# New engine and rank tables for the list scheduler of a two-layer hybrid backbone, and a price for PE's changes of tile shape

## The chip, the cores and the metric

The kernel runs on one core of one Trainium2 chip. The metric is the device time of one launch in microseconds. The core's engines each work through an instruction stream of their own in program order: TensorE (PE, with its weight loads listed as PEld), VectorE (DVE), ScalarE (ACT), GpSimd (POOL) and SyncE (SP), which issues the DMAs. They meet at semaphores.

## The reference, cut to what matters

Two layers work on 1024 latent tokens and 256 context tokens of width 1024, all in float32.

```python
for i in range(DEPTH):                                # 2 layers
    sh1, sc1, ga1, sh2, sc2, ga2 = split(silu(c) @ w_ada[i] + b_ada[i], 6)     # the context has its own
    hx = rms_norm(x, g_mix[i]) * (1 + sc1) + sh1      # hc the same from ctx
    zx = hx @ w_in[i]                                 # columns: q 512, k 128, v 128, pooling 256, Fourier 256
    q = apply_rope(head_rms(q, q_gain)); k = apply_rope(head_rms(k, k_gain))
    mx = concat([softmax(q k^T / 8) v over context + latent keys,    # 8 query heads of 64, 2 key heads
                 pool_mix(...), fourier_mix(...)])
    x = x + ga1 * (mx @ w_out[i])
    fx = rms_norm(x, g_ffn[i]) * (1 + sc2) + sh2
    gate, up = split(fx @ w_gate_up[i])               # 2816 columns each
    x = x + ga2 * ((silu(gate) * up) @ w_down[i])
    # layer 0 does the same for ctx, whose queries see context keys alone
return x
```

## The kernel before

Each large float32 product is made of three products of rounded halves, low by high, high by low, high by high (`mm3`, L485 to L487), summed in PSUM. So an operand is needed twice: as its rounded copy (the high half: a cast, `copy` at L472 on ACT and DVE, L470 on POOL) and as the remainder (the low half: a subtraction, `combine` at L475, on DVE or POOL). Weights come by DMA in tiles `hs` (output projection), `wst` (input projection, gate/up, down; `w` holds halves of them), `ast` (modulation). Some products are done in seven instead of eight partial products, for which sums of weight tiles and of inputs are made first (`ws`). The halves lie in `half`, `parts` and `w`.

A layer runs through input projection (`ps_in`), with the Fourier and pooling mixers; attention; output projection (`ps_o`) with the residual at L1883; gate and up (`ps_s`, `ps_m`, `ps_c` for the context); and down projection (`ps_d`, residual L2351). Between these, products for the modulation of the next steps (`ps_ada`, L591, 128 by 32 tiles) are put in.

Attention goes over blocks of 128 queries, and in each over four heads at a time, twice. Four heads are two pairs, and each head has 256 context keys and 1024 latent keys. The steps and their names are:

- SC, SA, SB: score products on PE (L1537), `ps_sc` for context keys, `ps_s` for latent keys
- MC, ML: row maxima on DVE (L1548, L1450); N: the exponential's bias on DVE (L1454)
- EC, EL: exponentials on ACT (L1460 into `pc` or `pd`, L1466 into `p`), with the row sums; EL gives back the score area in PSUM
- R: sum and reciprocal on DVE (L1554, L1555)
- Y and Z: scaling of `pc`/`pd` (128x256) and of `p` (128x1024) by the reciprocal (L1473 on ACT, L1475 on DVE or POOL)
- T: transposes on PE (L1488) into `ps_t`; C: copies `pt<-ps_t` (L472)
- V: products with the values on PE (L1512, 128 by 64 tiles) into `ps_pv`, in two runs per four heads; O: copy `mix<-ps_pv`

The order is found by a list scheduler in the kernel's own Python, the class `Plan`. Every step is recorded as an operation with a duration from a formula, what it comes after, and the buffers it takes and gives back. Its rank is a due time plus an entry of `SHIFTS` for its layer and name. Some kinds of step (copies, subtractions, scalings) may run on several engines: `ENGINES` lists these by the step's name (A for ACT, D for DVE, G for POOL). `run()` then keeps a clock for each engine, picks the step that can start first, of those that start nearly together the one with the lowest rank, gives it the engine on which it would start, and emits it. Steps on DVE and POOL exclude each other in that plan (`held`) unless named in `ALONE`. The hardware knows nothing of the plan's times: the instructions run in the order emitted on each engine, and wait for semaphores.

A run of value products is charged `4 * len(bs) * ns_fp32(256) + NS_MODE`, where `NS_MODE` stands for what PE loses when it changes from 128 by 128 tiles to other ones and back.

Of the kernel before, what the change touches and what calls it, by code (L numbers as in the profile page):

```python
# [39 lines left out]
H = {256: [f"h{k}" for k in range(8)], 768: [f"h{k}" for k in range(8, 16)], 0: [f"h{k}" for k in range(16, 20)]}  # L40
# [3 lines left out]
C = ("c0", "c1", "c2", "c3")  # L44
# [8 lines left out]
class Plan:  # L53
# [12 lines left out]
    SLACK = 60  # L66
    WINDOW = 40
# [38 lines left out]
    def run(self):  # L106
# [58 lines left out]
        pick = strict = True  # L165
        place = {e: k for k, e in enumerate(("PE", "A", "D", "G", "S", "N"))}
        while left:
# [26 lines left out]
            at, _, o, got, e = pick  # L194
            for b in o.can:
                ready[b].remove(o)
            o.engine, o.ns = e, o.can[e]
            by = o.engine
# [56 lines left out]
NS_MODE = 350  # L255
# [21 lines left out]
def setting(table, name, default):  # L277
# [6 lines left out]
             T=5.9, C=-12.1, H=-63.6, G=-21.5, V=6.3, F=6.6, O=-117.4, A=-149.8, X=-3.3)  # L284
# [6 lines left out]
ENGINES = {"C": "AD", "G": "G", "H": "ADG", "O": "A", "Y": "AD", "Z": "ADG", "act hi": "A", "act lo": "DG", "act sum": "D",  # L291
# [6 lines left out]
           "mix sum": "DG", "norm hi": "ADG", "norm lo": "G", "norm shift": "ADG", "out hi": "A", "out lo": "DG",  # L298
# [4 lines left out]

SHIFTS = ({"C": 919100, "EC": -545700, "EL": -1073100, "MC": -4100900, "ML": 314500, "N": -759500, "O": -2444400,
           "R": -2036600, "SA": 235500, "SB": -740400, "SC": -579700, "T": -221600, "V": -416700, "Y": 278400,
           "Z": 895000, "aa": -841600, "act hi": -1263600, "act lo": -1492900, "act sum": 1970600, "ada": -662600,
           "ada add": -132000, "ada row": -2031800, "ada sum": 1686900, "ada total": -365600, "ada turn": -1712000,
           "as": 1429200, "channels": -726100, "dft": -3497700, "dft alt": 1352500, "dft alt out": -676500,
           "dft copy": 1691400, "dft ctx": -1491300, "dft ctx out": -1510600, "dft out": 768100, "down": 1481200,
# [2187 lines left out]
```

## Time and profile before

| | |
|---|---|
| median of 3 runs | 2603.08 us (2601.51 to 2606.92) |
| profiled execution | 2608.01 us, span 2605.9 us |
| granted TensorE clock, mean | 0.991 |
| busy: PE, PEld | 2531.5 us (97%), 2092.5 us (80%) |
| busy: DVE, ACT, POOL | 2091.2 us (80%), 1253.5 us (48%), 540.2 us (21%) |
| chain that ended last | PE 78%, DVE 14%, ACT 3%, DMA 2%, issue 2% |

The span is what the profiler's records cover; the profiled execution's time is 2.1 us more, and the timed runs are executions without the profiler. A busy share is an average over stages with different limits, so that a stage's own limit is read from a window. In the 40 slices of the page PE stands at 9 tenths or more nearly throughout; the layer-0 stages end, read from the tiles written, near 238 us (input projection), 515 (attention), 615 (output projection), 1205 (gate and up), and layer 1's attention runs from about 1630 to 1870.

### The profile page before, as it was taken

The numbers are of one execution on the slowest core, as the hardware profiler recorded it, in microseconds if no ns is written. First come the engines' busy times: TensorE is split into PE (matmuls) and PEld (weight loads), VectorE is DVE, ScalarE is ACT, GpSimd is POOL, SyncE is SP. The second block draws the span as 40 slices with busy tenths as digits, with TensorE's granted clock in tenths as the row PEclk, the third lists the DMA queues.
The fourth block names the chain that finished last, engine by engine and source line by source line (L and its number), as shares of the span: only waits on it lengthen the run. The fifth ranks groups of instructions, "written<-read, shape, count | busy, mean of one in ns | idle before, by whom it ended". The sixth has DMA issues, their size and how long they took to land.

```text
span 2605.9 us, 38612 instructions
## 1 busy us (share of the span) xinstructions
PE 2531.5 (97%) x14382; PEld 2092.5 (80%) x14382; DVE 2091.2 (80%) x3466; ACT 1253.5 (48%) x2319; POOL 540.2 (21%) x450
## 2 busy tenths in 40 slices
PE   6999999998999999999999999999998999999999
PEld 5887777787788888888888988777776888888887
DVE  6766877799866998876788987877799977777886
ACT  4324888746322222224444533899746333334442
POOL 2022222122200000000223313322132311111241
PEclk9999999999999999999999999999998999999999
DMA  8243200354224455448434333100352423225733
GB/s 296 84 130 109 75 1 1 114 182 131 96 91 146 154 164 169 145 156 291 148 97 125 105 93 101 39 1 1 99 183 87 158 107 115 81 98 213 231 95 124
DMA packets 126203, 314.83 MB, mean 121 GB/s; under 512 B 14784, under 2 KB 23360, under 8 KB 126016
## 3 DMA queue, kind: packets, MB, share of 16 engines
q1 hardware_dynamic: 126016, 312.36, 36.4%
q8 instruction: 114, 1.87, 0.3%
q14 instruction: 73, 0.60, 0.1%
HBM read 244.94 MB, written 62.13 MB: 118 GB/s over the span
## 4 chain that ended last, share of the span: by engine, by line
PE 78%; DVE 14%; ACT 3%; DMA 2%; issue 2%; POOL 0%; SPq 0%; DVEq 0%; ACTq 0%; POOLq 0%
PE ps_s L485 8%; PE ps_s L486 8%; PE ps_s L487 8%; PE ps_d L485 6%; PE ps_d L486 6%; PE ps_d L487 6%; PE ps_pv L1512 5%; PE ps_t L1488 4%; PE ps_s L1537 4%; DVE half L475 3%; PE ps_in L485 3%; PE ps_in L486 3%; PE ps_in L487 3%; DVE x L1883 2%; DVE ws L475 1%
## 5 line engine op out<-in xcount | busy, mean ns | idle before, releaser
L472 ACT CAST half<-ws 128x512 fp32r<-128x512 f32 x404 | 243.9, 620 | 524.0 <-PE ps_s L487 236.6
L486 PE MATMUL ps_s<-half 128*128 128x512 f32 x1056 | 413.8, 392 | 6.4 <-DVE half L475 6.4
L485 PE MATMUL ps_s<-half 128*128 128x512 f32 x1056 | 414.8, 393 | 3.2 <-ACT half L472 2.6
L487 PE MATMUL ps_s<-half 128*128 128x512 f32 x1056 | 412.5, 391 | 0.0
L485 PE MATMUL ps_d<-half 128*128 128x512 f32 (+1 forms) x792 | 290.7, 367 | 2.0 <-ACT half L472 2.0
L486 PE MATMUL ps_d<-half 128*128 128x512 f32 (+1 forms) x792 | 290.2, 366 | 0.5 <-DVE half L475 0.5
L487 PE MATMUL ps_d<-half 128*128 128x512 f32 (+1 forms) x792 | 290.1, 366 | 0.0
L475 DVE TENSOR_TENSOR half<-ws,half 128x512 fp32r<-128x512 f32 x354 | 243.2, 706 | 56.6 <-ACT half L472 55.2
L486 PEld LDWEIGHTS ps_s<-half 128*128 128x128 f32 x1056 | 199.4, 189 | 50.7 <-DVE half L475 9.0
L485 PEld LDWEIGHTS ps_s<-half 128*128 128x128 f32 x1056 | 199.2, 189 | 46.6 <-ACT half L472 3.4
L487 PEld LDWEIGHTS ps_s<-half 128*128 128x128 f32 x1056 | 199.4, 189 | 41.6
L472 ACT CAST half<-wst 128x512 fp32r<-128x512 f32 x224 | 132.6, 618 | 163.9 <-PE ps_s L487 82.8
L475 POOL TENSOR_TENSOR ws<-wst 128x512 f32<-128x512 f32 x72 | 107.2, 1489 | 500.2 <-DVE half L475 413.8
L475 DVE TENSOR_TENSOR ws<-wst 128x512 f32<-128x512 f32 x258 | 173.4, 689 | 9.6 <-DMA wst<-in_w_gate_up 4.9
L475 DVE TENSOR_TENSOR half<-wst,half 128x512 fp32r<-128x512 f32 x204 | 152.3, 770 | 35.8 <-ACT half L472 35.6
L485 PEld LDWEIGHTS ps_d<-half 128*128 128x128 f32 x792 | 150.1, 190 | 26.7 <-ACT half L472 2.4
L486 PEld LDWEIGHTS ps_d<-half 128*128 128x128 f32 x792 | 150.1, 190 | 24.8 <-DVE half L475 0.7
L475 POOL TENSOR_TENSOR half<-ws,half 128x512 fp32r<-128x512 f32 x56 | 76.5, 1365 | 449.8 <-ACT half L472 396.2
L487 PEld LDWEIGHTS ps_d<-half 128*128 128x128 f32 x792 | 150.0, 189 | 24.0
L1450 DVE TENSOR_REDUCE smalls<-ps_s 128x1 f32<-128x1024 f32 x128 | 153.9, 1213 | 10.1 <-PE ps_s L1537 10.0
L485 PE MATMUL ps_in<-parts,w 128*128 128x512 f32 (+1 forms) x416 | 158.8, 382 | 1.6 <-ACT parts L472 1.6
L1512 PE MATMUL ps_pv<-pt,v 128*64 128x256 f32 x1312 | 156.4, 384 | 0.0
(284 smaller groups left out, 5874.0 us busy)
## 6 DMA issues: line engine op xcount, KB each, us to landing
wst<-in_w_gate_up SPq DMA_DIRECT2D x99, 512.0 KB, 4.3
ast<-in_w_ada SPq DMA_DIRECT2D x96, 512.0 KB, 3.7
as<-act_spill SPq DMA_DIRECT2D x165, 256.0 KB, 2.7
hs<-in_w_out SPq DMA_DIRECT2D x96, 256.0 KB, 3.0
act_spill<-c SPq DMA_DIRECT2D x44, 512.0 KB, 4.1
wst<-in_w_down SPq DMA_DIRECT2D x44, 512.0 KB, 6.4
x_spill<-x SPq DMA_DIRECT2D x28, 512.0 KB, 3.1
x<-x_spill SPq DMA_DIRECT2D x26, 512.0 KB, 6.5
```

What stands on the lines that cost most here:

```text
L472: (nc.scalar.copy if e == "A" else nc.vector.tensor_copy)(out, x)
L475: (nc.vector if e == "D" else nc.gpsimd).tensor_tensor(out, x, y, op)
L485: nc.tensor.matmul(o, wl, xh, start=start, stop=False)
L486: nc.tensor.matmul(o, wh, xl, start=False, stop=False)
L487: nc.tensor.matmul(o, wh, xh, start=False, stop=stop)
L1450: nc.vector.tensor_reduce(self.pair.col(1, self.h), self.s, AX.X, ALU.max)
L1488: nc.tensor.transpose(self.t[:, 2 * q + h, :], src, ident)
L1512: nc.tensor.matmul(self.bank[own], v[:, own], self.pt[k0][:, g, 2 * P * q:2 * P * q + 2 * P], start=(k0 + q == 0), stop=(k0 + q == self.nk ...
L1537: nc.tensor.matmul(o, self.q[0][:, self.h0 + h, :], kv["k", k0](self.g, j), start=(j == 1), stop=(j == 0))
L1883: nc.vector.scalar_tensor_tensor(v, o(), s, v, ALU.mult, ALU.add)
```

## The change

The change has three parts. The scheduler charges 300 ns (`SWITCH`) whenever PE goes from ordinary steps to one named in `PARTED`, and again when it goes back; `NS_MODE` falls from 350 to 50. The table `ENGINES` is new: the scaling of p (Z) may run on POOL alone, where it could run on ACT, DVE or POOL; the copy of attention results (O) may run on DVE too; `act sum` may go to POOL, `norm lo` goes from POOL to DVE, the high halves of the seventh and eighth columns of the input projection go to DVE, and others gain or lose an engine. Both tables of `SHIFTS`, one for a layer, are new in nearly every entry. What is computed stays the same.

```diff
+    SWITCH = 300
+    PARTED = ("ada", "V")
...
         pick = strict = True
+        parted = False
...
             o.engine, o.ns = e, o.can[e]
+            if e == "PE" and (o.name in Plan.PARTED) != parted:
+                parted, o.ns = not parted, o.ns + Plan.SWITCH
...
-NS_MODE = 350
+NS_MODE = 50
...
-ENGINES = {"C": "AD", "G": "G", "H": "ADG", "O": "A", "Y": "AD", "Z": "ADG", "act hi": "A", "act lo": "DG", "act sum": "D",
+ENGINES = {"C": "AD", "G": "G", "H": "ADG", "O": "AD", "Y": "AD", "Z": "G", "act hi": "A", "act lo": "DG", "act sum": "DG",
...
-           "R": -2036600, "SA": 235500, "SB": -740400, "SC": -579700, "T": -221600, "V": -416700, "Y": 278400,
-           "Z": 895000, "aa": -841600, "act hi": -1263600, "act lo": -1492900, "act sum": 1970600, "ada": -662600,
+SHIFTS = ({"C": 240000, "EC": -323700, "EL": -2200800, "MC": -481500, "ML": -539000, "N": -522600, "O": -598400, "R": -494400,
+           "SA": -45800, "SB": -1660200, "SC": -2264600, "T": -45500, "V": -777500, "Y": 141800, "Z": 256000,
```

In the changed kernel lines stand 3 to 6 later than before (L1466 is L1472, L1473 is L1479, L1475 is L1481, L475 is L481).

The first place is the steady part of layer 0's attention. On ACT, before, between two exponentials of latent scores:

```order
L1466 ACTIVATE p,smalls<-ps_s,smalls,rq 128x1024
L1473 ACTIVATE pd<-pd,smalls 128x256 x2
L1473 ACTIVATE p<-p,smalls 128x1024
L472 COPY mix<-ps_pv 128x2x128
L1460 ACTIVATE pc,smalls<-ps_sc,smalls,rq 128x256
L472 COPY pt<-ps_t 128x512
L1466 ACTIVATE p,smalls<-ps_s,smalls,rq 128x1024
```

And on ACT in the changed kernel:

```order
L1472 ACTIVATE p,smalls<-ps_s,smalls,rq 128x1024
L1479 ACTIVATE pd<-pd,smalls 128x256
L478 COPY mix<-ps_pv 128x2x128
L1466 ACTIVATE pc,smalls<-ps_sc,smalls,rq 128x256
L478 COPY pt<-ps_t 128x512
L1472 ACTIVATE p,smalls<-ps_s,smalls,rq 128x1024
L478 COPY pt<-ps_t 128x512 x2
```

The scaling of p is gone from ACT, and one of the two scalings of `pd`; POOL's stream has two scalings of p for each pair instead. On DVE at the same place, before:

```order
L1454 SCALAR_TENSOR_TENSOR smalls<-smalls,nrq 128x1
L1450 TENSOR_REDUCE smalls<-ps_s 128x1
L1475 TENSOR_SCALAR p<-p,smalls 128x1024
L1454 SCALAR_TENSOR_TENSOR smalls<-smalls,nrq 128x1
L472 CAST qt<-mix 64x256 x2
L472 COPY pt<-ps_t 128x512 x2
L1548 TENSOR_REDUCE smalls<-ps_sc 128x2
L1554 TENSOR_TENSOR smalls<-smalls 128x2
L1555 RECIPROCAL smalls<-smalls 128x2
L1450 TENSOR_REDUCE smalls<-ps_s 128x1
L1454 SCALAR_TENSOR_TENSOR smalls<-smalls,nrq 128x1
```

And on DVE in the changed kernel:

```order
L1561 RECIPROCAL smalls<-smalls 128x2
L1460 SCALAR_TENSOR_TENSOR smalls<-smalls,nrq 128x1
L1456 TENSOR_REDUCE smalls<-ps_s 128x1
L478 CAST qt<-mix 64x256 x2
L1460 SCALAR_TENSOR_TENSOR smalls<-smalls,nrq 128x1
L478 COPY pt<-ps_t 128x512 x2
L1554 TENSOR_REDUCE smalls<-ps_sc 128x2
L1456 TENSOR_REDUCE smalls<-ps_s 128x1
L1560 TENSOR_TENSOR smalls<-smalls 128x2
L1561 RECIPROCAL smalls<-smalls 128x2
L1460 SCALAR_TENSOR_TENSOR smalls<-smalls,nrq 128x1
```

The row maximum, which stood between the reciprocal and the bias, now stands ahead of the reciprocal, and the scaling of p is gone from DVE.

The second place is POOL from layer 0's output projection to its first gate products (`hs` and `wst` are weights as loaded, `ws` sums of them or of inputs). Before:

```order
L470 TENSOR_SCALAR w<-wst 128x512 x2
L470 TENSOR_SCALAR half<-x 128x512
L470 TENSOR_SCALAR w<-wst 128x512
L475 TENSOR_TENSOR ws<-x 128x512 x2
L470 TENSOR_SCALAR half<-ws 128x512
L470 TENSOR_SCALAR w<-wst 128x512 x2
L470 TENSOR_SCALAR half<-x 128x512
L475 TENSOR_TENSOR ws<-x 128x512
L470 TENSOR_SCALAR half<-x 128x512
L470 TENSOR_SCALAR half<-ws 128x512
```

And in the changed kernel:

```order
L481 TENSOR_TENSOR half<-hs,half 128x512
L481 TENSOR_TENSOR parts<-mix,parts 128x256
L481 TENSOR_TENSOR half<-hs,half 128x512 x4
L481 TENSOR_TENSOR half<-ws,half 128x512
L481 TENSOR_TENSOR half<-wst,half 128x512
L481 TENSOR_TENSOR half<-ws,half 128x512
L481 TENSOR_TENSOR half<-wst,half 128x512 x7
L481 TENSOR_TENSOR half<-ws,half 128x512
```

Casts (one input) and sums of x have left POOL for ACT and DVE, and subtractions (two inputs) have come from DVE.

The third place is PE at the entry of layer 0's attention, from the last score products among the input projection's. Before:

```order
L1537 MATMUL ps_s<-kd,qs 128x512 x8
L591 MATMUL ps_ada<-ast,cond 32x128 x8
L1031 MATMUL ps_v<-ident,vf 128x128 x6
L1537 MATMUL ps_sc<-kd,qs 128x256 x4
L604 MATMUL ps_at<-ident,rows 128x8
L1031 MATMUL ps_v<-ident,vf 128x128 x4
L1537 MATMUL ps_s<-kd,qs 128x512 x4
L1488 MATMUL ps_t<-ident,pc 128x128 x4
L591 MATMUL ps_ada<-ast,cond 32x128 x8
L1488 MATMUL ps_t<-ident,p 128x128 x12
```

And in the changed kernel:

```order
L1543 MATMUL ps_sc<-kd,qs 128x256 x4
L597 MATMUL ps_ada<-ast,cond 32x128 x8
L1494 MATMUL ps_t<-ident,pc 128x128 x4
L1543 MATMUL ps_s<-kd,qs 128x512 x4
L491 MATMUL ps_in<-parts,w 128x512
L492 MATMUL ps_in<-parts,w 128x512
L493 MATMUL ps_in<-parts,w 128x512
L491 MATMUL ps_in<-parts,w 128x512
L492 MATMUL ps_in<-parts,w 128x512
L493 MATMUL ps_in<-parts,w 128x512
L1494 MATMUL ps_t<-ident,p 128x128 x8
```

Six products of the input projection, which stood ahead of the last of these scores, now stand between scores and the first transposes of p.

## Rows read from the trace of the kernel before

**Rows 1.** The page: busy time of each engine, and the chain that ended last by engine.

```profile
PE 2531.5 (97%) x14382; PEld 2092.5 (80%) x14382; DVE 2091.2 (80%) x3466; ACT 1253.5 (48%) x2319; POOL 540.2 (21%) x450
...
PE 78%; DVE 14%; ACT 3%; DMA 2%; issue 2%; POOL 0%; SPq 0%; DVEq 0%; ACTq 0%; POOLq 0%
```

**Rows 2.** Windows by stage: length, busy us (instructions) of each engine, clock, DMA share, GB/s.

```profile
238.00:272.00 34.00, 31.46 (x248) 22.73 (x248) 29.47 (x57) 26.08 (x51) 8.14 (x9) 1.00 0.31 102
272.00:480.00 208.00, 203.67 (x1462) 149.24 (x1461) 163.15 (x316) 181.96 (x384) 50.76 (x52) 1.00 0.08 25
560.00:690.00 130.00, 115.84 (x626) 98.29 (x625) 126.94 (x200) 73.13 (x116) 36.20 (x30) 0.96 0.41 132
1630.00:1665.00 35.00, 30.07 (x181) 23.20 (x181) 32.69 (x64) 29.45 (x60) 13.85 (x16) 1.00 0.20 62
1665.00:1870.00 205.00, 205.00 (x1528) 158.11 (x1524) 151.85 (x303) 191.85 (x393) 45.46 (x47) 1.00 0.05 18
```

**Rows 3.** Score products (L1537), 270 to 480: idle before them until what (us, times).

```profile
  ACT p L1466: 14.3, 37
```

**Rows 4.** Timeline of ACT in both attentions: start, us, instruction.

```profile
318.20 1.14 ACT L1473 ACTIVATE p<-p,smalls 128x1024 f32<-128x1024 f32 x1
320.51 1.21 ACT L1466 ACTIVATE p<-ps_s,smalls,rq 128x1024 f32<-128x1024 f32 x1
...
482.47 1.14 ACT L1473 ACTIVATE p<-p,smalls 128x1024 f32<-128x1024 f32 x1
...
1684.86 1.14 ACT L1473 ACTIVATE p<-p,smalls 128x1024 f32<-128x1024 f32 x1
...
1853.03 1.14 ACT L1473 ACTIVATE p<-p,smalls 128x1024 f32<-128x1024 f32 x1
```

**Rows 5.** Scalings of p: count, duration min/median/max in ns, first and last start.

```profile
L1473 ACT ACTIVATE p<-p,smalls x50: 1133/1138/1181, 251.2 to 1859.0; 128x1024 f32<-128x1024 f32 x50
...
L1475 POOL TENSOR_SCALAR p<-p,smalls x62: 1118/1121/1324, 250.7 to 1852.0; 128x1024 f32<-128x1024 f32 x62
```

**Rows 6.** Timeline of POOL and DVE near 318 us.

```profile
317.48 1.12 POOL L1475 TENSOR_SCALAR p<-p,smalls 128x1024 f32<-128x1024 f32 x1 [4.34 <-DVE smalls L1555]
...
318.45 0.22 DVE L1454 SCALAR_TENSOR_TENSOR smalls<-smalls,nrq 128x1 f32<-128x1 f32 x1
```

**Rows 7.** Waits of PEld in 238:272, of PE in 1630:1665: total, times, longest.

```profile
PEld ps_t L1488 <- DVE pt L472: 2.2, 3, 1.0
PEld ps_s L1537 <- ACT p L1466: 1.4, 3, 0.8
...
PE ps_t L1488 <- ACT pc L1473: 1.4, 2, 0.8
PE ps_s L1537 <- ACT p L1466: 1.1, 2, 0.9
```

**Rows 8.** Timeline of PE in 596 to 664, with idle before.

```profile
602.38 0.39 PE L485 MATMUL ps_o<-parts,w 128*128 128x256 f32 x1 [2.14 <-DVE w L475]
...
660.00 0.50 PE L485 MATMUL ps_s<-half 128*128 128x512 f32 x1 [2.12 <-ACT half L472]
```

**Rows 9.** Timeline of DVE and POOL near 605 us.

```profile
604.66 1.28 DVE L475 TENSOR_TENSOR half<-ws,half 128x512 fp32r<-128x512 f32 x2
...
609.85 1.70 DVE L475 TENSOR_TENSOR half<-ws,half 128x512 fp32r<-128x512 f32 x2
...
609.37 1.04 POOL L470 TENSOR_SCALAR w<-wst 128x512 fp32r<-128x512 f32 x1 [8.19 <-DVE w L475]
```

**Rows 10.** The page's groups: POOL's low halves of sums of weights, mean ns of one.

```profile
L475 POOL TENSOR_TENSOR half<-ws,half 128x512 fp32r<-128x512 f32 x56 | 76.5, 1365 | 449.8 <-ACT half L472 396.2
```

**Rows 11.** Waits of PEld over the span: total us, times, longest.

```profile
PEld ps_pv L1512 <- issue: 19.2, 63, 0.4
PEld ps_t L1488 <- issue: 13.4, 36, 0.4
```

**Rows 12.** The page's DMA issues: count, KB each, median us to landing.

```profile
as<-act_spill SPq DMA_DIRECT2D x165, 256.0 KB, 2.7
```

67 lines of the change are left out of this document (33 added, 34 removed), and 67 rows, old and new, of tables (ENGINES, SHIFTS).

## The prediction

> **What bounds the kernel now.** I read the page's busy shares first, and there the reader should see that TensorE (PE) is at work 97% of the span and makes 78% of the chain that ended last [rows 1]. The change alters no arithmetic and nearly no PE order, so it can only win back time in which PE stands. I therefore cut the span into stages by the windows view [rows 2] and looked for stretches where PE is busy for less than the window. The second attention (1665 to 1870) is full: 205.00 of 205. The first (272 to 480) lacks 4.3 us, its entry (238 to 272) 2.5, the entry of the second (1630 to 1665) 4.9, and the stretch from layer 0's output projection into its gate/up (560 to 690) 14.2. In that last one VectorE (DVE) is busy 126.94 of 130, so it is DVE's stretch; the granted clock there is 0.96, so that part of it ran at the lower of the two levels (1.2 GHz), after PE had stood.
>
> Third came the waits of PE and of its weight loads. In the first attention the score products wait for ScalarE (ACT) to finish the exponential, because a score area comes free only then: 14.3 us in 37 waits [rows 3]. That figure holds waits of weight loads, which matmuls still in flight cover in part, so a second measure is wanted: the period of four heads, taken from ACT's scalings of p [rows 4]. From 318.20 to 482.47 there are 11 periods in 164.27 us, 14.93 each; in the second attention 12 periods take 168.17 us (1684.86 to 1853.03), 14.01 each, for the same work per period. So the first loses 0.92 us per period, and over some 14 periods about 13 us. That is the largest single loss the change can reach.
>
> **The change part by part.**
>
> *Scaling of p (step Z).* Now ACT does 50, DVE 16 and POOL 62 of the 128; the change gives POOL all. ACT sheds 50 x 1.138 = 57 us, POOL gains 66 x 1.12 = 74 us [rows 5]. On ACT the removed instruction stands between the reciprocal and the next exponential: it runs from 318.20 to 319.34, three short pieces follow, and the exponential that PE is waiting for starts at 320.51 [rows 4]. Without it the exponential can come up to 1.1 us earlier, which is more than the 0.92 us that a period loses. Bounds: 0 (another wait takes over) and -13 (the first attention runs at the pace of the second). I take -11, nearer to the period than to zero, because nothing else in rows 3 and 4 holds PE there, and keep 2 us for the odd wait that is left.
>
> *What POOL's pair of scalings makes late.* The two heads of a pair were scaled side by side, now one after the other: POOL began at 317.48 [rows 6], so a second one behind it would end 2 x 1.12 us later, at 319.72, where ACT's ended at 319.34. So the second scaled p comes some 0.4 us later than now, and POOL is busy only 50.76 of 208 us there. Queued behind the pair on POOL are the low halves of the next queries, which are not wanted in the same period. I cost it at 0. Its cover is that other PE work stands between scaling and transposes; without that cover it would cost up to 0.4 us for each of 64 pairs.
>
> *The port.* Of two DVE subtractions, 128x512 each, the pair at 604.66 took 1.28 us alone and the pair at 609.85 took 1.70 us beside a POOL cast that began at 609.37 [rows 9]: 0.42 us were lost to one POOL instruction. In attention the DVE instruction that could suffer is the exponential's bias (L1454, two SBUF inputs). At 318.45 it started just as POOL's scaling ended (317.48 + 1.12 = 318.60) and took 0.22 us [rows 6]. With a second scaling behind it, it could wait 1.12 us more. In the new order the bias stands right behind the reciprocal after 51 of the 72, before POOL has begun (in the old one after 15); so I take 0 here and keep the other outcome as a rival. The Trainium skill ("SBUF — State Buffer", section "SBUF: two separate sides") says that POOL and a DVE instruction with two SBUF inputs exclude each other for a whole instruction. The 0.42 us lost in rows 9 agree in kind; by the rule in full a bias that meets the pair would lose up to 2.24 us.
>
> *Entry of the first attention.* Here PE waits for copies of transposes on DVE (2.2 us of weight-load waits) and for the exponential (1.4) [rows 7]. The new order puts the last input projections between the first scores and the first transposes, and neither engine carries scalings of p. Bounds 0 and -5; I take -3.5, since these two rows make 3.6.
>
> *Entry of the second attention.* PE waits 1.4 us for ACT's scaling of pc and 1.1 for the exponential [rows 7]; both stand behind scalings of p that go. The rest of the 4.9 us (a cast of V and copies) is not touched. Bounds 0 and -4.9; I take -2.5, the sum of the two.
>
> *Output projection into gate/up, layer 0.* The stands before 602.38 (2.14 us, weights' low halves on DVE) and 660.00 (2.12, a high half on ACT) [rows 8] are what a late DVE, or an ACT queued behind it, looks like. From the first residual to the first gate product I count on DVE 18 low halves fewer (10 of `ws`, 7 of `wst`, 1 of `hs`) and 6 sums more, and small pieces (casts, copies, context parts) that come to -0.7 us. At 0.64 us each (1.28 / 2 [rows 9]) this is -11.5 + 3.8 - 0.7 = -8.4 us. POOL keeps 35 instructions in that stretch, but 17 casts and sums of 0.6 to 1.5 us become low halves of 1365 ns [rows 10], and beside a longer POOL instruction DVE loses more: at half of 0.42 us, 17 x 0.21 = 3.6. Net -4.8; I take -5. Bounds: -14 (all of PE's stand in rows 2) and +4 (each of the 9 low halves of `ws` that POOL gets is late by its own 1365 ns, 12.3 us, against the 8.4 won). ACT gets 14 casts more there, some 8.7 us, in a stretch where it is busy 73 of 130; it hides them.
>
> *The planner's price for a change of PE's tile shape.* The old plan added 350 ns to each run of value products; the new one adds 50, and 300 at each change in or out. What the trace charges is a wait of 0.30 us before a run (19.2 / 63) and 0.37 behind it (13.4 / 36) [rows 11]. In the new order there are still 67 runs of value products, and 37 runs of modulation products instead of 40. So this edit by itself saves at most 3 x 0.67 = 2.0 us; I take -1. The Trainium skill ("TensorEngine Tiling (Array Packing)", section "Key Properties") says that a change of tiling mode drains TensorE; the two waits of rows 11 agree, and by the rule the gain hangs on the number of changes, which hardly moves.
>
> *Everything else that is reordered* (input projections, down projections, the second gate/up). There I find no stall removed and some risks: the norm's sums of the context come after 78 instead of 54 output products, and at the start of layer 1's down projection SyncE has the last stores among the loads, where a load takes 2.7 us to land [rows 12]. Bounds 0 and +8 (three such landings); I take +3, about one.
>
> **Sum.** Against the profiled run, 2608.01 us (span 2605.9): -11 - 3.5 - 2.5 - 5 - 1 + 3 = -20, so 2588.0. That run lies 4.9 us above the median of the three timed (2603.08), so in terms of the median 2583. The likeliest case has a range of its own, 2570 to 2596.
>
> **Rivals.**
>
> *A wait takes the place of the exponential's.* In the second attention ACT scales p too (1684.86 [rows 4]), is busy 191.85 of 205 us, and PE never stands [rows 2]. So a scaling on ACT does not cost by itself; the place of it does, and another order may have another bad place: a transpose waiting for POOL's second scaling, or a copy. Then both attentions and their entries gain nothing: 2608.0 - 5 - 1 + 3 - 4.9 = 2600, no measurable change. Against it: nothing now waits long for POOL, and ACT loses 57 us of work. Chance 0.15.
>
> *Slower: the bias behind POOL's pair.* If DVE's bias, in the place where it stands now (318.45), meets the second scaling, it and the exponential come 1.12 us later, against a mean of about 0.57 us that ACT wins per pair. That is 0.55 us late for each of 64 pairs, 35 us if PE has no other work, some 18 with half of it covered: 2600 + 18 = 2618. For it speaks that the second attention has no slack on PE to give. Against it, the bias's place in the new order. It decides from the point where bias rows start behind the second scaling's end. This is also what the skill's rule of exclusion would bring. Chance 0.11.
>
> *More than I count.* The first attention reaches the pace of the second (-13), both entries close (-5, -4.9), the projection's stand goes (-14), no new wait comes, the switches give 2: 2608.0 - 38.9 - 4.9 = 2564. Against it: DVE stays near full from 560 on. Chance 0.12.
>
> *The change doesn't do what it says.* The price of switching leaves the runs of value products at 67; taken alone it is worth 1 us, within what can't be told. This lies inside the second case's time; it becomes the result only if the new tables win nothing either.
>
> **How the numbers follow.** My forecast has 0.62, "more" 0.12, no gain 0.15, slower 0.11. A measurement of this kernel can tell about 0.2% (5.2 us) from no change. Faster is the forecast and "more", 0.74; same is 0.15; slower 0.11. The range of 8 in 10 leaves out the slower case and the lower half of "more": from 2562, just under its 2564, to 2604, which takes in the no-gain case.
>
> **What would show it.** Right: all 128 scalings of p on POOL near 1.12 us; the period of four heads in the first attention falls from 14.93 to about 14.1; score products there wait under 4 us for the exponential; PE's stand from 560 to 690 falls from 14.2 to about 9; runs of value products cost as before. Wrong: bias rows of about 1 us or starting behind the second scaling, transposes waiting for POOL, a period in the second attention above 14.01, or new stands where layer 1's down projection begins.

## The result and the profile after

The changed kernel takes 2627.14 us (median of 4, 2623.94 to 2635.80) against 2602.77 (median of 4): a ratio of 1.0089, 95% interval 1.0075 to 1.0104. It is slower by 24 us, where 20 us faster was forecast. The profiled run took 2627.5 us; its span of 2625.7 us is 19.8 longer than the span before. The missing 4.6 us comes mostly from the profiled run of before, which lay 5.2 above its median.

The page's busy line and its chain by engine:

```profile
PE 2538.8 (97%) x14382; PEld 2087.4 (79%) x14382; DVE 2124.3 (81%) x3432; ACT 1219.8 (46%) x2286; POOL 625.2 (24%) x517
...
PE 71%; DVE 19%; DMA 5%; ACT 3%; issue 2%; SPq 0%; POOL 0%; DVEq 0%; ACTq 0%; POOLq 0%
```

Against [rows 1], work moved the way that was forecast: ACT lost 34 us and POOL won 85 (57 and 74 were forecast for the scalings alone). The share of DVE in the chain rose from 14% to 19%. Next, the places on PE's timeline where a stage begins or ends, read from its tiles in both traces:

| stretch, us | before | after | difference | forecast |
|---|---|---|---|---|
| start to first value products | 272.52 | 274.57 | +2.05 | -3.5 |
| layer 0's attention, first to last value product | 245.46 | 246.72 | +1.26 | -11 |
| on to the first gate product | 101.01 | 93.57 | -7.43 | -5 |
| gate/up, layer 0 | 585.60 | 588.82 | +3.22 | 0 |
| down projection, then to layer 1's first value products | 452.60 | 452.91 | +0.31 | -2.5 |
| layer 1's attention | 214.20 | 228.88 | +14.68 | 0 |
| on to the first gate product | 80.98 | 79.60 | -1.38 | 0 |
| gate/up, layer 1 | 439.11 | 443.88 | +4.77 | 0 |
| down projection and end | 214.45 | 216.74 | +2.29 | 0 |

The forecast's -1 for the price and +3 for everything else were not placed in a stretch. Layer 1's attention alone lost 14.7 us; layer 0's did not win its 11. The windows that answer to [rows 2], same columns (the last runs to 1880 here):

```profile
272.00:480.00 208.00, 203.81 (x1478) 149.18 (x1477) 173.15 (x319) 157.36 (x342) 86.93 (x82) 1.00 0.09 28
560.00:690.00 130.00, 117.88 (x641) 98.00 (x640) 125.91 (x193) 80.66 (x130) 38.81 (x23) 0.97 0.42 136
...
1665.00:1880.00 215.00, 212.58 (x1516) 156.51 (x1516) 175.55 (x318) 161.54 (x352) 81.87 (x80) 1.00 0.04 15
```

In layer 1's attention PE is no longer full. ACT fell from 191.85 us in 205 to 161.54 in 215, so it is not short of time; what it does comes too late. The period of four heads, read from POOL's scalings of p at the same phase (start, us, instruction):

```profile
1693.19 2.29 POOL L1481 TENSOR_SCALAR p<-p,smalls 128x1024 f32<-128x1024 f32 x2 [3.13 <-DVE smalls L1460]
...
1855.37 2.22 POOL L1481 TENSOR_SCALAR p<-p,smalls 128x1024 f32<-128x1024 f32 x2 [4.33 <-DVE smalls L1460]
```

These stand 11 periods apart, 14.74 us each, where [rows 4] gave 14.01. Waits of weight loads in that stretch (total us, times, longest), after and then before:

```profile
PEld ps_t L1494 <- issue: 10.9, 28, 0.5
PEld ps_pv L1518 <- issue: 10.5, 29, 0.4
PEld ps_sc L1543 <- ACT pd L1466: 3.7, 7, 0.6
PEld ps_t L1494 <- DVE pt L478: 2.2, 11, 0.4
PEld ps_sc L1543 <- ACT pc L1466: 1.5, 6, 0.7
PEld ps_s L1543 <- ACT p L1472: 1.4, 4, 0.3
PEld ps_t L1494 <- ACT pt L478: 0.9, 4, 0.2
```

```profile
PEld ps_pv L1512 <- issue: 7.5, 29, 0.4
PEld ps_t L1488 <- issue: 4.2, 11, 0.4
PEld ps_sc L1537 <- ACT pc L1460: 2.7, 7, 0.4
PEld ps_sc L1537 <- ACT pd L1460: 2.3, 6, 0.4
PEld ps_t L1488 <- DVE smalls L1450: 1.2, 3, 0.4
```

Besides the two lines of "issue" (changes of tile shape) the reader sees many short waits after the change: context scores for the context exponential, which gives back their one PSUM bank, score areas for the latent exponential, transposes for copies. Before, context scores show 13 waits too, but of another kind, as weight loads of PE at one place in each order show:

```profile
1713.25 2.36 PEld L1512 LDWEIGHTS ps_pv<-pt,v 128*64 128x64 f32 x24 [0.17 <-issue]
1715.99 0.53 PEld L1537 LDWEIGHTS ps_sc<-kd,qt 128*128 128x128 f32 x4 [0.38 <-ACT pd L1460]
```

```profile
1715.07 2.36 PEld L1518 LDWEIGHTS ps_pv<-pt,v 128*64 128x64 f32 x24 [0.37 <-issue]
1717.82 0.42 PEld L1494 LDWEIGHTS ps_t<-ident,p 128*128 128x128 f32 x4 [0.39 <-issue]
1719.58 0.53 PEld L1543 LDWEIGHTS ps_sc<-kd,qt 128*128 128x128 f32 x4 [0.64 <-ACT pd L1466]
```

Before, the context scores stood right behind the long run of value products, and each of their 13 waits is 0.38 us, as long as any other wait behind such a run: it is the change of tile shape, whoever is named. After, transposes take that wait, and what the context scores wait (5.2 us in all) comes on top; so do 3.1 us for copies and 1.4 for score areas. The lines of "issue" are no part of the loss, though they grew from 11.7 to 21.4 us. Behind the runs the wait only has another name now. Ahead of a run it is 0.17 us behind transposes and 0.36 behind latent scores, whose single product is longer; but from the last product's start to the run's first, PE takes 0.09 us more than between two products of the same kind in either case (0.20 against 0.11, 0.33 against 0.24).

How a wait for the exponential arises, from DVE, POOL, ACT and PE:

```profile
1716.78 1.38 DVE L478 CAST qs<-mix 64x256 fp32r<-64x256 f32 x2
1718.19 0.65 DVE L1460 SCALAR_TENSOR_TENSOR smalls<-smalls,nrq 128x1 f32<-128x1 f32 x1
...
1715.69 2.32 POOL L1481 TENSOR_SCALAR p<-p,smalls 128x1024 f32<-128x1024 f32 x2 [2.68 <-DVE smalls L1460]
...
1718.87 0.57 ACT L1466 ACTIVATE pd<-ps_sc,smalls,rq 128x256 f32<-128x256 f32 x1 [0.65 <-DVE smalls L1460]
...
1719.58 0.74 PE L1543 MATMUL ps_sc<-kd,qt 128*128 128x256 f32 x4 [0.21 <-ACT pd L1466]
```

Two casts beside POOL's pair take 1.38 us, the bias behind them 0.65, the exponential waits for it, and PE for the exponential. In groups of DVE over layer 1's attention (count, busy us, mean ns), after and then before:

```profile
L1460 DVE SCALAR_TENSOR_TENSOR smalls<-smalls,nrq 128x1 f32<-128x1 f32 x53 | 18.9, 357 | 0.7
L478 DVE CAST qt<-mix 64x256 fp32r<-64x256 f32 x12 | 5.6, 502 | 0.1
```

```profile
L1454 DVE SCALAR_TENSOR_TENSOR smalls<-smalls,nrq 128x1 f32<-128x1 f32 x53 | 10.1, 211 | 0.2
L472 DVE CAST qt<-mix 64x256 fp32r<-64x256 f32 x12 | 2.9, 283 | 0.1
```

So the first theory (P) was the slower rival: POOL's pair holds DVE, and that makes the loss. The experiments were to show whether it is the whole of it. The rival theory (O) is that the new order costs the time, whoever scales. "Same order" below means that each step was planned as before and only the instruction put out differs; then all engines' orders stay but for the steps named.

### The profile page after: what moved, and what is told of

Its sections match the earlier page's. It is cut to its first block, busy times and chain, and to the rows that moved or that the text cites. A ratio compares the mean times of both kernels' runs of the same rounds, so it can differ in the third digit from the quotient of the medians.

```text
span 2625.7 us, 38731 instructions
## 1 busy us (share of the span) xinstructions
PE 2538.8 (97%) x14382; PEld 2087.4 (79%) x14382; DVE 2124.3 (81%) x3432; ACT 1219.8 (46%) x2286; POOL 625.2 (24%) x517
## 4 chain that ended last, share of the span: by engine, by line
PE 71%; DVE 19%; DMA 5%; ACT 3%; issue 2%; SPq 0%; POOL 0%; DVEq 0%; ACTq 0%; POOLq 0%
PE ps_s L491 7%; PE ps_s L492 7%; PE ps_s L493 7%; PE ps_d L492 5%; PE ps_d L491 5%; PE ps_d L493 5%; DVE half L481 4%; PE ps_t L1494 4%; PE ps_pv L1518 4%; PE ps_s L1543 3%; PE ps_in L491 3%; PE ps_in L492 3%; PE ps_in L493 3%; DVE ws L481 2%; DMA ast<-in_w_ada 2%; DVE x L1889 2%
## 5 line engine op out<-in xcount | busy, mean ns | idle before, releaser
L481 DVE TENSOR_TENSOR half<-ws,half 128x512 fp32r<-128x512 f32 x332 | 239.6, 725 | 56.5 <-ACT half L478 55.2
L481 POOL TENSOR_TENSOR half<-ws,half 128x512 fp32r<-128x512 f32 x78 | 114.5, 1468 | 521.1 <-ACT half L478 443.2
L481 DVE TENSOR_TENSOR ws<-wst 128x512 f32<-128x512 f32 x278 | 212.7, 769 | 20.6 <-DMA wst<-in_w_gate_up 12.4
L1481 POOL TENSOR_SCALAR p<-p,smalls 128x1024 f32<-128x1024 f32 x128 | 146.4, 1155 | 253.1 <-DVE smalls L1460 210.2
L481 POOL TENSOR_TENSOR ws<-wst 128x512 f32<-128x512 f32 x52 | 75.1, 1445 | 490.0 <-DVE half L481 342.4
```

Source lines behind the costliest of these rows:

```text
L481: (nc.vector if e == "D" else nc.gpsimd).tensor_tensor(out, x, y, op)
L1481: (nc.vector if e == "D" else nc.gpsimd).tensor_scalar(x, x, r, 0.0, ALU.mult, ALU.add)
```

## Experiments

In the tables, periods are the mean of ten, from DVE's row maxima (every fourth); "attention" is first to last value product.

| kernel | period, layer 0 / 1 | attention 0 / 1, us | median, us |
|---|---|---|---|
| before | 14.93 / 14.01 | 245.5 / 214.2 | 2602.77 to 2605.24 |
| after | 14.75 / 14.75 | 246.7 / 228.9 | 2627.14 |
| z_second_on_act | 16.37 / 16.42 | 264.9 / 252.4 | 2674.93 |
| before_z_on_pool | 14.72 / 14.02 | 243.8 / 214.2 | 2604.80 |
| bias_one_input | 14.56 / 14.56 | 240.5 / 226.2 | 2625.31 |
| before_l0_z_on_dve | 14.75 / 14.01 | 244.6 / 214.2 | 2605.85 |
| before_l0_ranks_of_l1 | 14.05 / 14.02 | 230.2 / 214.2 | 2618.39 |
| before_l1_ranks_of_l0 | 14.93 / 17.72 | 245.5 / 274.0 | 2659.53 |
| after_l1_cycle_of_before | 14.70 / 15.13 | 243.2 / 245.2 | 2641.83 |
| after_old_price | 14.70 / 14.57 | 244.1 / 227.2 | 2626.44 |
| after_short_scaling | 14.61 / 14.61 | 242.0 / 227.0 | 2629.24 |
| before_short_scaling | 14.66 / 14.01 | 242.1 / 214.1 | 2600.97 |
| after_z_in_quarters | 14.75 / 14.74 | 243.6 / 228.2 | 2631.64 |
| before_z_on_pool_quarters | 14.70 / 14.01 | 243.5 / 214.1 | 2603.10 |
| after_v_later_l1 | 14.75 / 14.72 | 244.3 / 229.5 | 2634.13 |
| after_v_later_both | 14.64 / 14.72 | 243.7 / 230.0 | 2631.56 |
| before_v_later_l0 | 15.26 / 14.01 | 249.2 / 214.2 | 2610.31 |
| before_v_uneven_l1 | 14.93 / 17.12 | 245.6 / 254.7 | 2645.64 |

### Where the scaling runs

**The new order, second head's scaling on ACT.**

```diff
                 r = self.pair.col(5, self.h)
+                if e == "G" and self.h == 1:
+                    e = "A"
```

> The changed kernel with its order of emission kept, but the scaling of p for the second head of each pair (64 of 128) issued to ACT instead of POOL. Theory P (port): POOL's two scalings in a row hold up DVE's two-input bias (mean 357 ns in layer 1's attention, 211 before) and the query casts; with one scaling the bias falls below 250 ns, the period of four heads from 14.65 to about 14.1 us in both attentions, and the time by 10 to 16 us to 2611 to 2617. Rival O (order): the new order of scores, values and transposes itself costs the 14 us in layer 1's attention; then the period stays at 14.5 or more, ACT gets 73 us of work back, and the time is 2625 to 2635.

2674.93 us, ratio 1.0274 (1.0253 to 1.0295). The bias got shorter (layer 1's mean is 269 ns, 355 in the changed kernel), and yet the period rose to 16.4 us. Theory P falls as it stood. In the new order ACT cannot take half of the scalings without loss; in the old order of layer 1 it had 30 of 64, and the next run shows that this cost nothing there.

**The old order, all scalings on POOL.**

```diff
                 r = self.pair.col(5, self.h)
+                if x is getattr(self, "p", None):
+                    e = "G"
```

> The kernel before with its order kept, but all 128 scalings of p issued to POOL. Theory P: the bias behind POOL's pair gets longer, the period of four heads in layer 1's attention rises from 14.01 to 14.4 or more, the gain from ACT's relief in layer 0 is eaten, and the time is 2608 to 2618. Rival O: without the order nothing is lost: layer 0's attention gains up to 11 us as predicted, layer 1's stays at 14.01, and the time is 2592 to 2603.

2604.80 us, ratio 0.9995 (0.9984 to 1.0007). Layer 1's period stays at 14.02, although the bias there gets longer much as it does in the changed kernel (mean 308 ns in 54, before 211):

```profile
L1454 DVE SCALAR_TENSOR_TENSOR smalls<-smalls,nrq 128x1 f32<-128x1 f32 x54 | 15.6, 308 | 0.3
```

So POOL's pair costs nothing in that order. Layer 0's period falls only from 14.93 to 14.72. One place in its trace where ACT's relief does not reach PE (POOL, DVE, ACT, PE):

```profile
330.49 2.21 POOL L1477 TENSOR_SCALAR p<-p,smalls 128x1024 f32<-128x1024 f32 x2 [1.61 <-DVE smalls L1557]
...
331.79 0.92 DVE L1454 SCALAR_TENSOR_TENSOR smalls<-smalls,nrq 128x1 f32<-128x1 f32 x1
...
332.74 0.56 ACT L1460 ACTIVATE pc<-ps_sc,smalls,rq 128x256 f32<-128x256 f32 x1 [0.71 <-DVE smalls L1454]
...
335.12 1.21 PE L1539 MATMUL ps_s<-kd,qt 128*128 128x512 f32 x4 [0.54 <-ACT p L1466]
```

The bias ends at 332.71, as POOL's pair does (332.70); ACT, free of its scaling, waits 0.71 us for it, and PE still waits for the exponential behind it.

**The old order, layer 0's ACT scalings on DVE.**

```diff
                 r = self.pair.col(5, self.h)
+                if e == "A" and l == 0 and x is getattr(self, "p", None):
+                    e = "D"
```

> The kernel before with its order kept, but those scalings of p in layer 0 that ACT did issued to DVE. If the scaling in front of the exponential is what PE waits for in layer 0's attention, as the prediction held, the period of four heads there falls from 14.93 to about 14.1 us and the time by 8 to 11 us to 2592 to 2595. If its place on ACT was not the cause, or DVE gets late by it, the period stays at 14.8 or more and the time at 2600 or above.

2605.85 us, ratio 1.0005 (0.9995 to 1.0015); the period goes to 14.75. On DVE the scaling stands ahead of the bias. On POOL, on DVE, or left out but for a sixteenth (below), layer 0's period lies between 14.66 and 14.75, so the scaling's place on ACT was not the cause that I took it for. The counts could have told it: of its 64 scalings layer 0 had 20 on ACT, the faster layer 1 had 30.

### How long the scaling and the bias take

**Scalings cut to 64 columns, both orders.** The rest of p is left unscaled.

```diff
                 r = self.pair.col(5, self.h)
+                if x is getattr(self, "p", None):
+                    x = x[:, :64]
```

> The changed kernel with its order kept, each scaling of p cut to its first 64 of 1024 columns (the rest of p stays unscaled, so this leaves out work). Theory PO (order and port together): the new order puts the bias, and with it both exponentials, behind POOL's scalings, so the port's hold goes into the period; with short scalings the period of four heads is 14.0 to 14.3 us in both layers and the time 2606 to 2616. Rival O (the order by itself, whoever scales and however long): the period stays at 14.55 or more and the time at 2622 or above.

> The kernel before with the same cut (64 of 1024 columns scaled, the rest left out), order and engines kept. Theory PO: layer 0's order has the exponentials behind a scaling on whatever engine, so its period falls from 14.93 to 14.0 to 14.3 us and layer 1's stays at 14.01; time 2592 to 2597. Rival O: layer 0 stays at 14.6 or more, time 2600 or above.

After: 2629.24 us, ratio 1.0097 (1.0078 to 1.0116), period 14.61 in both layers. Before: 2600.97 us, 0.9988 (0.9978 to 0.9997), period 14.66 and 14.01. A scaling now takes 0.32 us on POOL and 0.33 on ACT, instead of 1.12 and 1.14. That is worth 0.14 us per period in the new order and 0.27 in layer 0's old one; the rest, some 0.6 us, is there with the short ones. Rival O's forecast holds in both.

**Bias with one input.**

```diff
-                nc.vector.scalar_tensor_tensor(pr.col(2, h), pr.col(0, h), pr.col(1, h), nrq[...], ALU.max, ALU.mult)
+                nc.vector.tensor_scalar(pr.col(2, h), pr.col(0, h), pr.col(1, h), nrq[...], ALU.max, ALU.mult)
```

> The changed kernel with the exponential's bias on DVE written as one input and two per-partition scalars instead of two inputs and a scalar; nothing else is changed. Theory P in its narrow form (two SBUF inputs meet POOL's port): the bias no longer waits (mean back near 210 ns), and the time falls by 4 to 10 us to 2617 to 2623, the query casts still held. Theory P in a wide form (any SBUF-reading DVE instruction of this size is held): bias and time as in the changed kernel, 2627 within 3. Rival O: the same 2627 even where the bias gets shorter.

2625.31 us, 1.0080 (1.0059 to 1.0101). All 128 of the bias at L1460 now take 252 to 276 ns, beside POOL's work or not (in the changed kernel 199 to 1105): this form takes longer by itself but is not held. The period fell to 14.56; the time did not move beyond its interval. So the bias's holds are real and worth 0.2 us a period, not 0.74. The casts of the queries are still held here.

**Scalings in quarters, both orders** (in the old one all on POOL, by the two lines shown above).

```diff
-                    (nc.vector if e == "D" else nc.gpsimd).tensor_scalar(x, x, r, 0.0, ALU.mult, ALU.add)
+                    for k in range(0, x.shape[-1], 256):
+                        y = x[:, k:k + 256]
+                        (nc.vector if e == "D" else nc.gpsimd).tensor_scalar(y, y, r, 0.0, ALU.mult, ALU.add)
```

> The changed kernel with each scaling of p on POOL cut into four instructions of 256 columns, all of p scaled, order kept. Theory PO: a DVE instruction that meets POOL waits for a quarter instead of a whole scaling, the bias's mean falls from 354 to under 280 ns, the period from 14.75 to 14.4 to 14.6 us and the time by 2 to 8 us to 2619 to 2625. Rival: the scalings follow each other without a gap for DVE or cost more in all; period 14.7 or more, time 2626 or above.

> The kernel before, order kept, all scalings of p on POOL and in four instructions each. With whole scalings layer 0's period was 14.72 us and the time that of the kernel before. Theory PO: layer 0 falls to 14.3 to 14.6, layer 1 stays at 14.0, time 2597 to 2602. Rival: 14.7 or more and 2604 or above.

2631.64 us, 1.0110 (1.0086 to 1.0134), and 2603.10 us, 1.0000 (0.9990 to 1.0009). Periods are as with whole scalings, though layer 1's bias fell from a mean of 355 to 285 ns in the new order. Nothing is won.

### The order

**Layer 1's attention ranks in layer 0, and the other way round** (the kernel before; 18 entries such as V and Z taken from the other layer's table; two of them shown, of the first kernel).

```diff
-SHIFTS[0]: "V": -416700, ... "Z": 895000
+SHIFTS[0]: "V": 511700, ... "Z": 813100
```

> The kernel before with its 18 attention entries of the rank table of layer 0 replaced by those of layer 1, so that layer 0's attention runs PE in layer 1's cycle (24 value products, context scores, transposes, two score groups, 16 value products, ...), Z still on ACT, DVE and POOL. Theory C (cycle): the period of four heads follows the cycle on PE, not the engine of Z; layer 0 goes from 14.93 to about 14.0 us and the time to 2589 to 2596. Theory P (port and engine of Z): the period stays near 14.9 and the time within 4 us of the kernel before.

> The kernel before with its attention entries of layer 1 replaced by those of layer 0, engines of Z as before. Theory C: layer 1's period rises from 14.01 to 14.6 or more and the time by 8 to 14 us to 2612 to 2619. Theory P: no scaling is moved to POOL by more than a few, so the period stays near 14.0 and the time within 4 us of the kernel before.

With layer 1's ranks layer 0's period is 14.05, its attention 15 us shorter, and PE full there:

```profile
300.00:450.00 150.00, 149.92 (x1113) 115.76 (x1111) 117.74 (x235) 143.73 (x295) 38.18 (x39) 1.00 0.01 3
```

PE's steady order there is layer 1's, and the scalings still run on POOL (31) and ACT (32, before 20), so the order does this by itself. The second kernel is slower, 2659.53 us, 1.0213 (1.0197 to 1.0228), and layer 1's period is 17.72; its order on PE came out as neither of the two (in each period two context scores follow each other with no value run between them), so that it does not show what layer 0's order costs in layer 1. The first kernel was nevertheless slower too, 2618.39 us, 1.0062 (1.0045 to 1.0079). Its gate/up in layer 0 takes 606.8 us instead of 585.6, and a window of it shows where the gain went; this kernel, then before:

```profile
640.00:1200.00 560.00, 545.35 (x2964) 467.10 (x2963) 434.96 (x650) 159.52 (x276) 46.11 (x29) 0.98 0.40 135
```

```profile
640.00:1200.00 560.00, 554.96 (x3084) 477.57 (x3084) 449.13 (x675) 169.48 (x290) 52.45 (x34) 1.00 0.43 142
```

PE stands 14.7 us instead of 5.0 and ran part of the stretch at the lower clock level after such stands (0.98 against 1.00). The planner had also put that stage's DVE steps in another order, and PE waits for halves there (13.2 us in the window, before 3.4), as here:

```profile
827.02 0.80 PE L485 MATMUL ps_s<-half 128*128 128x512 f32 x1 [3.18 <-DVE half L475]
```

**Old ranks, engines and price in layer 1 of the changed kernel; and the old price alone.**

```diff
+    may = {"Z": "ADG", "O": "A"}[name] if self.layer == 1 and name in ("Z", "O") else setting(...)   # first kernel only
-    SWITCH = 300
+    SWITCH = 0
-NS_MODE = 50
+NS_MODE = 350
```

> The changed kernel with, in layer 1's attention, the old rank entries and the old engine lists of Z and O, and with the old price (350, no SWITCH): PE then has the old cycle in layer 1. Theory C: the period there is 14.0 again, the loss of 14 us in layer 1's attention goes, and the time is 2608 to 2617. If it stays above 2622, most of the loss is elsewhere than in the attention cycle.

> The changed kernel with the old price alone (NS_MODE 350, SWITCH 0), the new tables kept. The planner then spaces the two runs of value products in another way (about 3.4 us of other PE work behind the longer run, then some 6). Theory C: both layers' period changes with it, to 14.0 to 14.4, and the time falls by 8 to 20 us to 2607 to 2619. The prediction's view (the price is worth 1 us): 2624 to 2630.

2641.83 us, 1.0149 (1.0134 to 1.0164). The plan did not bring the old cycle back: over most of layer 1's attention PE's order repeats after eight heads and is neither the old one nor the new one, and periods of 14.06 and 17.8 us take turns. So this kernel does not test theory C, that PE's cycle sets the period, and no kernel puts the old cycle into the changed one. That PE's cycle does not set it alone is shown by z_second_on_act, which has the changed kernel's order on PE and a period of 16.4. The old price alone: 2626.44 us, 1.0086 (1.0071 to 1.0101); as the prediction had it, the price is worth nothing that can be told.

**One run of value products moved on PE.** In the first three kernels the shorter run comes one step later, and the copy of its result moves with it on ACT or DVE; in the last one the longer run does, in the old layer 1, and the orders of ACT, DVE and POOL stay as they were. The moves are made after the planning:

```diff
-            o.emit(...)
+            done.append((o, ...))
...
+        # each "V" of 2 (or, in the last kernel, 3) blocks goes behind the next "SB", its copy "O" with it; then all are emitted
```

> The changed kernel with one thing moved on PE: in layer 1's attention each run of 16 value products (trace count) comes one step later, behind the next eight transposes of p and the next score group, with its copy of the result behind it. Before the move 2.3 us of other PE work stand behind the run of 24 and 8 us behind the run of 16; after it 4.1 and 6.3. Theory E (value runs spaced evenly give copies and exponentials time): the period in layer 1 falls from 14.75 to 14.0 to 14.4 us, layer 0's stays, time 2617 to 2622. Rival D (DVE's and ACT's order decides, not PE's): the period stays at 14.6 or more, time 2624 or above.

> The same move in both layers of the changed kernel. Theory E: both periods 14.0 to 14.4 us, time 2607 to 2617. Rival D: both 14.6 or more, 2624 or above. What layer 0's attention wins may be given back in its output projection and gate/up, as it was with layer 1's ranks in layer 0.

> The kernel before with the same move in layer 0's attention alone; DVE's and POOL's orders are untouched. Theory E: the period there falls from 14.93 to 14.1 to 14.5 us and the time by 5 to 10 us to 2593 to 2598. Rival D: the period stays at 14.7 or more, time 2601 or above.

> The kernel before with, in layer 1's attention, each run of 24 value products moved one step later, behind the next context scores, transposes and score group; ACT's, DVE's and POOL's orders are untouched. The two runs then stand 1.8 and some 7 us apart instead of 4.1 and 5. Theory E: the period rises from 14.01 to 14.4 to 14.9 us and the time by 5 to 13 us to 2608 to 2617. Rival D: the period stays within 0.2 of 14.01 and the time at 2605 or below.

2634.13 us (1.0107, 1.0090 to 1.0124), 2631.56 (1.0100, 1.0085 to 1.0115), 2610.31 (1.0021, 1.0010 to 1.0031) and 2645.64 (1.0154, 1.0139 to 1.0169). Even spacing wins nothing: in the changed kernel 14.72 in layer 1 and 14.64 in layer 0, and layer 0 before gets worse. Theory E falls as a rule. But the last kernel, whose ACT, DVE and POOL orders are those of before, loses 3.1 us a period by one move on PE. PE's waits in layer 1's attention there:

```profile
PE ps_sc L1566 <- ACT pc L1489: 16.3, 7, 2.3
PE ps_sc L1566 <- ACT pd L1489: 14.1, 6, 2.3
```

In the old order the long run of value products stood right ahead of the context scores, and covered the time until the exponential had read their only bank. Taken away from there, it covers nothing, and PE stands up to 2.3 us, 30.4 in all. This is the link itself, not the changed kernel's loss: the new order costs 0.7 us a period, not 3.1.

None of these kernels beats the kernel before beyond its interval but the one that leaves work out.

## Why the prediction was wrong

**The step that failed** is the first: "The change alters no arithmetic and nearly no PE order, so it can only win back time in which PE stands." The counts of PE's rows were near, but in layer 1 the places were not. The old layer 1 had a cycle of its own: 24 value products, context scores, transposes, scores, 16 value products. The change puts both layers into the cycle that layer 0 had, but for one swap of scores: transposes and then context scores behind the long run, and the short run 2.5 to 2.8 us after it (in the old layer 1, 4.2). With that, "205.00 of 205" was not something to keep for nothing but a state of the order that was lost. Of the 14.68 us lost there, about 10 are in the period (14.74 against 14.01 over some 13) and 4 behind the last latent scores (22.80 us to the last value product, before 18.81; nothing here shows why). That the order does it and not the engine of Z is shown from both sides: the old order with all scalings on POOL keeps 14.02, the new one with scalings of 0.32 us keeps 14.61. Layer 0's old order with all scalings on POOL has 14.72, the changed kernel 14.75 in both layers. Weight loads' waits name the links: the context bank (5.2 us), the copies (3.1) and the score areas (1.4). Which single move of the new order would give the 0.6 us back stays open; moving the short run did not. The change also moved copies from ACT to DVE (76 of `pt` on DVE in the windows of the groups above, before 61, beside 53 biases each), and no run takes that apart from the order.

**Scaling of p, -11.** The row was right (the scaling stood in front of the exponential), the inference from it was not. The difference of the periods, 0.92 us, was taken for the cost of that instruction since both layers do the same work. Cutting it to 0.33 us is worth 0.27 us a period (14.93 to 14.66), 3.4 us over the attention, and moving it to POOL 0.21. The other 0.65 us was mostly layer 0's order: with layer 1's ranks its period is 14.05, with 32 scalings on ACT at their full length. The count of "11 periods, 12 periods" was the evidence for this, read the wrong way: the two layers differed in two things, and I saw one. In the changed kernel layer 0's period did fall, by 0.18 us, but from the last latent scores to the last value product it took 3.8 us more, as in layer 1.

**The port, 0.** Wrong in kind, small in size. The bias rose from 211 to 357 ns in layer 1's attention, and held ACT at 1718.87. A bias row of about 1 us, a sign of being wrong, did appear (up to 1105 ns). Standing behind the reciprocal did not save it, as the other bias of a pair comes later, here behind query casts that POOL holds too. The rival "slower: the bias behind POOL's pair" had the sign and nearly the time (2618), but its 18 us were not this: short scalings give back 0.14 us a period and no time. Its price also had a slip: 57 us of ACT's work in 64 pairs are 0.89 us a pair, not 0.57, and 0.23 us late in 64 pairs would be 15 us, not 35. The Trainium skill's rule ("SBUF — State Buffer", section "SBUF: two separate sides"), that POOL and a DVE instruction with two SBUF inputs exclude each other, agrees with 331.79 to 332.71, where the bias ended with POOL's pair; the 0.92 us there is POOL's remaining time, not a whole instruction.

**POOL's second scaling, 0.** Right: in layer 1's attention POOL held a transpose once, for 0.4 us.

**Entries.** Forecast -3.5 and -2.5, measured +2.05 (with the input projection) and +0.31 (with the down and input projections). PE's standing of 2.5 us in 238 to 272 became 4.8; in 1630 to 1665 it went from 4.9 to 5.6, and the mean granted clock from 1.00 to 0.95, part of it at the lower level. PE waited for exponentials there (2.9 and 1.5 us), the wait that was to go.

**Output projection into gate/up, -5.** Right in sign and size: -7.43 us to the first gate product, and -5.2 to the 200th product of gate/up (at 689.24 us before), near the end of the stretch that was forecast. Of its two stands [rows 8], the one for ACT's half is gone and the one for DVE's low halves of weights is 1.18 us now (before 607.34), but others came (1.55 us before 643.13, 1.74 before 652.82). Over the whole of layer 0's gate/up 3.22 us were given back.

**The price, -1.** Right: the old price gives 2626.44. Over the span, waits ahead of value runs are 23.4 us in 67, where [rows 11] has 19.2 in 63; what a change costs PE from start to start stayed (see above), and so did the count of value runs, 67. The Trainium skill ("TensorEngine Tiling (Array Packing)", section "Key Properties") says that a change of tiling mode drains TensorE; the trace agrees with a wait of 0.38 us behind each value run, before and after.

**Everything else, +3.** Measured +3.22 and +4.77 in the gate/up stages, -1.38 and +2.29 around: together about 9 us. In layer 1's gate/up 2.8 us are one wait, for squares of the norm that DVE had late (7.51 us, 4.71 before). What made the rest was not taken apart; PE's other long waits in gate/up are mostly for halves from DVE.

## What to carry to other kernels

Where a stage has no idle time on the bounding engine, a new order has little to win and can lose, here 14.7 us: bound such a stage by what the order around each shared buffer covers, not at zero. Two stages with the same work and different periods differ in everything that their orders differ in; cutting the instruction seen ahead of the waiting one from 1.14 us to 0.33 won 0.27 us of a period's 0.92. Compare orders by what stands between a buffer's release and its next use, not by counts of rows.

## What the runs showed of the hardware

One move on PE, with all other engines' orders kept, changed the period by 22% (14.01 to 17.12 us). An instruction of DVE on 128x1 elements with two inputs, 0.20 to 0.22 us otherwise, took 0.92 us beside a POOL instruction with one input, and a pair of casts 1.38 us (before, 0.50 us at 1714.79); cutting POOL's instruction in four (bias mean 285 ns instead of 355) gave no time back. With one tensor input the same bias took 252 to 276 ns in all 128 cases and was never held. A weight load behind a run of 128 by 64 tiles waited 0.38 us each time; ahead of such a run it waited 0.17 us behind products of 128 columns and 0.36 behind products of 512, at the same cost from start to start.
